# Mean squares of q and k taken token by token, with the squares as the stationary operand, in a two-layer encoder trunk

## The chip, the cores and the metric

The kernel runs on one core of a Trainium2 chip. The metric is the device time of one execution in microseconds (us), lower is better. Engines are named as in the profile: PE is TensorE's matmul, PEld its weight load, ACT is ScalarE, DVE is VectorE, POOL is GpSimd, and SP issues the DMAs.

## The reference

One sequence of 512 tokens with 1024 channels passes two residual layers. Layer 0 mixes with a gated convolution and a gated linear recurrence, layer 1 with stick-breaking attention in 16 heads of 64 channels; each is followed by an MLP with squared ReLU. The change touches only the QK-norm of layer 1:

```python
def mixer_stick_breaking(h, w_qkv, q_norm, k_norm, w_out):
    qkv = (h @ w_qkv).reshape(B, S, 3, SB_HEADS, SB_HEAD_DIM)
    q = rms_norm(qkv[:, :, 0], q_norm)
    k = rms_norm(qkv[:, :, 1], k_norm)
    ...
def rms_norm(x, g):
    y = xf * lax.rsqrt(jnp.mean(xf * xf, axis=-1, keepdims=True) + EPS)
```

So each token needs, for each head, the mean of 64 squares of q and the mean of 64 squares of k.

## The kernel before

Activations stand with channels on the 128 partitions and the 512 tokens along the columns. Weight products are written as three fp32r matmuls each (lines 281 to 283, and 1595 to 1597 for v): high part by high part, high by low, low by high. The attention layer works on pairs of heads: pair p (0 to 7) has its q in one tile of 128 channels (two heads of 64) by 512 tokens, and its k in another.

The attention stage isn't written in program order. `Graph` holds operations with an engine, a planned duration and their dependences; `Graph.run` places them one after the other by planned time, priority and ring slots, and what comes out is each engine's fixed order of instructions. A planned duration that changes can so move other operations, on any engine. Matmuls of weights form one chain that gives PE its filling; the rest, the attention units and the norms, is placed between them with priority 0 as soon as the plan says that it can start. Tiles that are used in turn come from rings: `miscs` is a ring of two PSUM banks, `nsqs` of two tiles of squares, `rows_` of one tile in SBUF.

For each pair: `q_evict` and `k_evict` take q and k out of PSUM, and among that write the squares (`nsq`, ACT). `mean_squares` forms the means and adds EPS into a 128 x 16 tile `m` of ring r0, which has tokens on the partitions and, along the columns, q or k (s), block of 128 tokens (b) and head (h). `qk_norm` takes the reciprocal root of m on DVE (`rsqrt_of`, lines 301 to 308), turns k's half back to rows and scales k. The attention units (`unit_z`, `unit_t`, `unit_a`) follow.

`mean_squares` before has four steps:

- line 1459, PE: for s = 0 and s = 1 a matmul whose stationary operand is `hs` (128 x 32, fp32: 1/64 in 16 columns for each head) and whose moving operand is the tile of squares (128 channels by 512 or 256 tokens). It leaves the means with tokens along the columns, 16 equal rows for each head, in partitions 64 to 127 of one bank. The compiler makes two matmul instructions of each such fp32 matmul.
- line 1461, ACT: a copy of these 64 rows from PSUM to the tile `rows`.
- line 1465, PE: one transpose of 64 x 128 for each block of 128 tokens, into a second bank.
- line 1468, DVE: EPS is added, and one of each 16 equal columns is kept, into m.

It is called ten times: for pairs 0 and 1 twice each with two blocks (tokens 0 to 255, then 256 to 511), and for pairs 2 to 7 once with four blocks (`qk_stream`).

Of the kernel before, what the change touches and what calls it, by code (L numbers as in the profile page):

```python
# [13 lines left out]
F32 = mybir.dt.float32  # L14
# [6 lines left out]
ALU = mybir.AluOpType  # L21
PSUM = bass.MemoryType.PSUM

P = 128
T = 512
NT = 8
EPS = 1e-6
# [184 lines left out]
def act_us(n, psum=False, column=False):  # L212

    return 0.094 + n * 0.000833 - 0.042 * psum + 0.093 * column


def dve_us(n):
    return 0.068 + n * 0.00104


def trunk(tc, x_d, c_d, rep_d, small_d, const_d, ada_d, ws_d, win_d, wv_d, woab_d, w1_d, w2_d, wqk_d, wvc_d, woc_d, out_d):
    nc = tc.nc
    act, dve, pool_e, pe, sync = nc.scalar, nc.vector, nc.gpsimd, nc.tensor, nc.sync
# [19 lines left out]
    ident = cons[:, C_ID:C_ID + P]  # L243
    ones = base.tile([P, P], F32, name="ones")
    o32 = cons[:, C_O32:C_O32 + 32]
    hs = cons[:, C_HS:C_HS + 32]
# [38 lines left out]
    def ks(k):  # L285
        return slice(k * P, (k + 1) * P)
# [975 lines left out]
    def ring(where, shape, dt, name, n=1):  # L1262

        return Ring(lambda k: (where() if callable(where) else where).tile(shape, dt, name=name, tag=name, bufs=n), n)

    def bank_ring(bs):
        r = Ring(lambda k: pp.tile([P, T], F32, name=f"b{bs[k]}", tag=f"b{bs[k]}"), len(bs))
        for k, b in enumerate(bs):
            if b in banks:
                r.slots[k] = tail[banks[b]]  # L1270
        return r
# [4 lines left out]
    miscs, accs, zts = bank_ring(free_b[:2]), bank_ring(free_b[2:4]), bank_ring(free_b[4:])  # L1276
# [7 lines left out]
    def in_ap(shape, dt, name, n=1):  # L1284
        r = ring(lambda: ap, shape, dt, name, n)
        ap_rings.append(r)
        return r
# [10 lines left out]
    oms, bes = [one_tile(om_t, i) for i in range(3)], [one_tile(be_t, i) for i in range(3)]  # L1298
    stqs, stks, kraws = in_ap([P, 1024], F32R, "stq", 5), in_ap([P, T], F32R, "stk", 6), in_ap([P, T], F32, "kraw", 3)
    vrs, oTs, krows = in_ap([P, 4, 256], F32, "v", 2), in_ap([P, T], F32R, "oT", 10), in_ap([4, T], F32R, "krow")  # L1300
    rows_ = in_ap([P, T], F32, "rows")
    rrs = [in_ap([P, 16], F32, f"r{i}", n) for i, n in enumerate((2, 1, 3, 3))]
    yts = in_ap([P, 16], F32R, "yt", 2)
    xh = {(o, hf): Handle() for o in range(NT) for hf in range(2)}
# [8 lines left out]
    def on_act(n, fn, r, w, prio=1, psum=False, column=False, **kw):  # L1313
        return G.op("ACT", act_us(n, psum, column), fn, r, w, prio, **kw)

    def on_dve(n, fn, r, w, prio=1, **kw):
        return G.op("DVE", dve_us(n), fn, r, w, prio, **kw)

    def on_pe(dur, fn, r, w, prio=0, **kw):
        return G.op("PE", dur, fn, r, w, prio, **kw)  # L1320
# [104 lines left out]
    QQ, KK, kraw, sqs, rq, oT, vs = {}, {}, {}, {}, {}, {}, {}  # L1425
# [18 lines left out]
    def k_evict(p, ps, cut, sl):  # L1444
# [4 lines left out]
        on_act(n, lambda: act.copy(kraw[p].t[:, sl], cut(ps.t)), (ps,), (kraw[p],), 0, psum=True)  # L1449
        on_act(n, lambda: act.activation(sq.t[:, sl], cut(ps.t), AF.Square), (ps,), (sq,), 0, psum=True)  # L1450

    def mean_squares(p, bs, s0):

        if bs[0] == 0:
            rq[p] = [rrs[i].new() for i in range(4)]
        ms, row, col, m = miscs.new(), rows_.new(), miscs.new(), rq[p][0]
        sl, n = slice(P * bs[0], P * bs[-1] + P), P * len(bs)
        for s in range(2):
            on_pe(0.13, lambda s=s, sq=sqs[p, s, s0]: pe.matmul(ms.t[64 + 32 * s:96 + 32 * s, sl], hs, sq.t[:, sl], start=True, stop=True),  # L1459
                  (sqs[p, s, s0],), (ms,), 0)  # L1460
        on_act(n, lambda: act.copy(row.t[64:, sl], ms.t[64:, sl]), (ms,), (row,), 0, psum=True)

        def flip():
            for b in bs:
                pe.transpose(col.t[:, 64 * b:64 * b + 64], row.t[64:, ks(b)], ident[64:, 64:])
        on_pe(0.08 * len(bs), flip, (row,), (col,), 0)
        bb = slice(bs[0], bs[-1] + 1)
        on_dve(16, lambda: dve.tensor_scalar(
            m.t.rearrange("p (s b h) -> p s b h", s=2, b=4)[:, :, bb],
            col.t[:, 0:256].rearrange("p (b s h r) -> p s b h r", b=4, s=2, h=2)[:, :, bb, :, 0], EPS, None, op0=ALU.add), (col,), (m,), 1)  # L1470

    def qk_norm(p):

# [97 lines left out]
    def qk_stream(p):  # L1571
        ops = []
        for s in range(2):
            w, ps = weights(wqk_d[p, s]), accs.new()
            ops += [mm3h(ps, whole, w, ks(k), (hh[0][k], hh[1][k]), FULL, k == 0, k == NT - 1, T) for k in range(NT)]
            (k_evict if s else q_evict)(p, ps, whole, FULL)
        mean_squares(p, (0, 1, 2, 3), 0)
        qk_norm(p)
        return ops
# [63 lines left out]
    for hf in range(2):  # L1643
        if hf:
            finish([nt_.acc[1]] + [nt_.sq[o, 1] for o in nin.direct], 1, 1, 0, (), [order[48 + 8]])
        ps = [r.new() for r in (accs, accs, zts, zts)]
        for k, s in by_half(hf, 4):
            order.append(mm3h(ps[s], half, w[s], ks(k), (hh[hf][k],), H[hf], k == 0, k == NT - 1, 256))
        for p in range(2):
            q_evict(p, ps[2 * p], half, H[hf])  # L1650
            k_evict(p, ps[2 * p + 1], half, H[hf])
            mean_squares(p, (2 * hf, 2 * hf + 1), 256 * hf)
# [11 lines left out]
    for s_ in "v0 q2 q3 u0 u1 v1 w0 q4 v2 q5 u2 q6 u3 q7 v3 u4 u6 w1 u5 u7".split():  # L1664
        n = int(s_[1])
# [140 lines left out]
```

## Time and profile before

| | |
|---|---|
| Median of 3 runs | 1243.63 us (1243.44 to 1245.4) |
| The profiled execution | 1245.21 us, of which the span from first to last instruction is 1243.4 us |
| PE busy | 1217.4 us, 98% of the span, 7649 matmul instructions |
| DVE busy | 890.5 us, 72% |
| ACT busy | 618.7 us, 50% |
| Mean granted clock of TensorE | 0.996 of full speed |
| HBM traffic | 127 GB/s over the span |

Matmuls are pipelined and the profile models their ends, so the duration of one instruction is longer than the time that it takes from PE. What a matmul takes is read from the start of it to the start of the next one. The mean squares lie between 622 and 826 us of the span.

### The profile page before, as it was taken

To read this page: it belongs to the slowest core of one execution; us is meant where nothing else is said; L and a number is where in the kernel's file an instruction comes from. 1 tells how busy PE (TensorE), PEld (TensorE's weight loads), DVE (VectorE), ACT (ScalarE), POOL (GpSimd) and SP (SyncE) were. 2 spreads that over 40 slices of the span, in tenths; PEclk is the share of its full clock that TensorE was granted. 3 is DMA by queue.
4 is the path that set the end of the run, shared out by engine and by line. 5 is a ranking of instruction groups with operands and counts; after the bars stand their busy time and mean duration, and the time that the engine had idled before them with its cause. 6 is when DMAs were issued, how large, how long until landed. Compare 5 with 4: busy or idle time off the path is not lost.

```text
span 1243.4 us, 19173 instructions
## 1 busy us (share of the span) xinstructions
PE 1217.4 (98%) x7649; PEld 1058.9 (85%) x7649; DVE 890.5 (72%) x1435; ACT 618.7 (50%) x1111; POOL 11.2 (1%) x24
## 2 busy tenths in 40 slices
PE   7999999989999999999999999999989999999998
PEld 6888877889899899898977877787878898998998
DVE  8996868769788687787857765568694585665761
ACT  4433233347256265274568655667465283472650
POOL 0000000000000000000300000000000000000000
PEclk9999999999999999999999999999999999999999
DMA  8764444623745727527332122323114223143141
GB/s 305 258 208 161 143 153 135 203 69 107 246 135 183 245 92 244 179 99 259 110 102 85 52 68 85 94 60 103 35 37 134 85 101 122 58 146 102 54 151 51
DMA packets 46618, 163.50 MB, mean 131 GB/s; under 512 B 5296, under 2 KB 6328, under 8 KB 46528
## 3 DMA queue, kind: packets, MB, share of 16 engines
q1 hardware_dynamic: 46384, 161.78, 39.5%
q8 instruction: 60, 0.98, 0.3%
q10 hardware_dynamic: 144, 0.49, 0.1%
q14 instruction: 30, 0.25, 0.1%
HBM read 155.96 MB, written 2.10 MB: 127 GB/s over the span
## 4 chain that ended last, share of the span: by engine, by line
PE 84%; DVE 8%; DMA 4%; ACT 2%; issue 1%; SPq 0%; DVEq 0%; ACTq 0%
PE b L281 20%; PE b L283 20%; PE b L282 20%; PE acc L281 3%; PE acc L283 3%; PE acc L282 3%; PE b L1539 2%; PE b L1560 1%; DMA raw<-in_ws 1%; PE b L1595 1%; PE b L1459 1%; DMA wraw<-in_w 1%; PE b L1596 1%; PE b L1597 1%; DVE wlo L272 1%
## 5 line engine op out<-in xcount | busy, mean ns | idle before, releaser
L271 ACT CAST whi<-wraw 128x1024 fp32r<-128x1024 f32 x125 | 130.0, 1048 | 217.9 <-DMA wraw<-in_w 87.7
L282 PE MATMUL b<-hidl,whi 128*128 128x512 f32 (+1 forms) x560 | 208.4, 372 | 1.0 <-DVE hidl L291 1.0
L281 PE MATMUL b<-hidh,whi 128*128 128x512 f32 (+1 forms) x560 | 208.6, 373 | 0.2
L283 PE MATMUL b<-hidh,wlo 128*128 128x512 f32 (+1 forms) x560 | 208.0, 371 | 0.0
L283 PE MATMUL b<-hh,wlo 128*128 128x256 f32 (+1 forms) x632 | 193.5, 306 | 7.1 <-DVE wlo L272 7.1
L281 PE MATMUL b<-hh,whi 128*128 128x256 f32 (+1 forms) x632 | 197.6, 313 | 2.0 <-ACT hh L1419 2.0
L282 PE MATMUL b<-hl,whi 128*128 128x256 f32 (+1 forms) x632 | 193.3, 306 | 1.2 <-DVE hl L1421 1.2
L272 DVE TENSOR_TENSOR wlo<-wraw,whi 128x1024 fp32r<-128x1024 f32 x125 | 152.1, 1222 | 58.8 <-ACT whi L271 57.6
L281 PEld LDWEIGHTS b<-hh,whi 128*128 128x128 f32 x632 | 120.4, 191 | 14.6 <-issue 7.2
L283 PEld LDWEIGHTS b<-hh,wlo 128*128 128x128 f32 x632 | 120.5, 191 | 13.3 <-DVE wlo L272 7.8
L282 PEld LDWEIGHTS b<-hl,whi 128*128 128x128 f32 x632 | 121.8, 193 | 6.2 <-DVE hl L1421 1.8
L282 PEld LDWEIGHTS b<-hidl,whi 128*128 128x128 f32 x560 | 105.6, 188 | 19.5 <-DVE hidl L291 1.6
L505 DVE SCALAR_TENSOR_TENSOR x<-b,modc,x 128x512 f32<-128x512 f32 (+1 forms) x102 | 68.2, 675 | 75.2 <-PE b L283 75.1
L281 PEld LDWEIGHTS b<-hidh,whi 128*128 128x128 f32 x560 | 105.2, 188 | 19.1 <-ACT hidh L290 1.0
L283 PEld LDWEIGHTS b<-hidh,wlo 128*128 128x128 f32 x560 | 105.2, 188 | 18.5
L419 DVE CUSTOM_DVE_ANT_0 wraw<-wraw,cb 128x1024 f32<-128x1024 f32 x80 | 97.4, 1221 | 26.3 <-DMA wraw<-in_ada 25.9
L272 DVE TENSOR_TENSOR wlo<-tt,whi 128x1024 fp32r<-128x1024 f32 x52 | 63.4, 1221 | 22.5 <-ACT whi L271 21.9
L271 ACT CAST whi<-tt 128x1024 fp32r<-128x1024 f32 x52 | 53.4, 1049 | 45.3 <-PE b L282 32.7
L1373 DVE TENSOR_TENSOR wlo<-raw,whi 128x1024 fp32r<-128x1024 f32 x34 | 41.6, 1222 | 23.6 <-ACT whi L1372 23.5
L291 DVE TENSOR_TENSOR hidl<-cm,hidh 128x256 fp32r<-128x256 f32 (+1 forms) x90 | 44.4, 510 | 18.5 <-ACT hidh L290 17.7
L281 PE MATMUL acc<-hh,whi 128*128 128x512 f32 x128 | 52.3, 408 | 0.0
L1523 DVE TENSOR_TENSOR_SCAN om<-om,pat 128x772 f32<-128x772 f32 (+2 forms) x24 | 46.5, 1936 | 5.8 <-ACT om L1519 5.8
(378 smaller groups left out, 2631.4 us busy)
## 6 DMA issues: line engine op xcount, KB each, us to landing
wraw<-in_w SPq DMA_DIRECT2D x124, 512.0 KB, 3.6
wraw<-in_ada SPq DMA_DIRECT2D x80, 512.0 KB, 4.3
eraw<-in_ada SPq DMA_DIRECT2D x16, 512.0 KB, 3.7
wraw<-in_win SPq DMA_DIRECT2D x16, 512.0 KB, 3.5
raw<-in_wqk SPq DMA_DIRECT2D x16, 512.0 KB, 4.1
raw<-in_ws SPq DMA_DIRECT2D x8, 512.0 KB, 6.0
wraw<-in_woab SPq DMA_DIRECT2D x8, 512.0 KB, 3.2
raw<-in_wvc SPq DMA_DIRECT2D x8, 512.0 KB, 3.3
```

The source lines that it names most:

```text
L271: act.copy(hi, raw)
L272: dve.tensor_tensor(lo, raw, hi.bitcast(F32), op=ALU.subtract)
L281: pe.matmul(ps, whi, h[0][:, hs], start=start, stop=False, **kw)
L282: pe.matmul(ps, whi, h[1][:, hs], start=False, stop=False, **kw)
L283: pe.matmul(ps, wlo, h[0][:, hs], start=False, stop=stop, **kw)
L291: dve.tensor_tensor(lo[:, sl], t_[:, sl], hi[:, sl].bitcast(F32), op=ALU.subtract)
L419: dve.tensor_tensor_reduce(out=raw, in0=raw, in1=cb, scale=1.0, scalar=0.0, op0=ALU.mult, op1=ALU.add, accum_out=modr[:, col:col + 1])
L505: dve.scalar_tensor_tensor(x[o][:, sl], ps, mcol(l, v, o), x[o][:, sl], op0=ALU.mult, op1=ALU.add)
L1373: on_dve(1024, lambda: dve.tensor_tensor(lo.t, raw.t, hi.t.bitcast(F32), op=ALU.subtract), (raw, hi), (lo,), 1)
L1459: on_pe(0.13, lambda s=s, sq=sqs[p, s, s0]: pe.matmul(ms.t[64 + 32 * s:96 + 32 * s, sl], hs, sq.t[:, sl], start=True, stop=True), (sqs[p, ...
L1523: on_dve(2 * nw, lambda: dve.tensor_tensor_scan(s_(), s_(), pats[i][:, ::-1], 0.0, op0=ALU.mult, op1=ALU.max), (om,), (om,), 2)
L1539: pe.transpose(tp.t[:, o_:o_ + P], be.t[:, w0:w0 + P], ident)
```

## The change

The squares become the stationary operand, a block of 128 tokens at a time, and the moving operand is two columns of `hs`, one for each head (columns 0 and 16). The product then has tokens on the partitions from the start, one column for each head, so that the copy, the tile `rows`, the second bank and the transposes go. All matmuls of a call are one operation of the plan, which needs both tiles of squares; its planned duration on PE is 0.22 us for each block of tokens, where the old steps had 0.13 us for each s and 0.08 us for each block.

```diff
-    rows_ = in_ap([P, T], F32, "rows")
...
+    hs2 = hs[:, 0:32:16]
+
     def mean_squares(p, bs, s0):
 
         if bs[0] == 0:
             rq[p] = [rrs[i].new() for i in range(4)]
-        ms, row, col, m = miscs.new(), rows_.new(), miscs.new(), rq[p][0]
-        sl, n = slice(P * bs[0], P * bs[-1] + P), P * len(bs)
-        for s in range(2):
-            on_pe(0.13, lambda s=s, sq=sqs[p, s, s0]: pe.matmul(ms.t[64 + 32 * s:96 + 32 * s, sl], hs, sq.t[:, sl], start=True, stop=True),
-                  (sqs[p, s, s0],), (ms,), 0)
-        on_act(n, lambda: act.copy(row.t[64:, sl], ms.t[64:, sl]), (ms,), (row,), 0, psum=True)
-
-        def flip():
-            for b in bs:
-                pe.transpose(col.t[:, 64 * b:64 * b + 64], row.t[64:, ks(b)], ident[64:, 64:])
-        on_pe(0.08 * len(bs), flip, (row,), (col,), 0)
+        col, m, sq = miscs.new(), rq[p][0], [sqs[p, s, s0] for s in range(2)]
+        view = lambda t_: t_.rearrange("p (s b h) -> p s b h", s=2, b=4)
+
+        def sums_of():
+            for s in range(2):
+                for b in bs:
+                    pe.matmul(col.t[:, 8 * s + 2 * b:8 * s + 2 * b + 2], sq[s].t[:, ks(b)], hs2, start=True, stop=True)
+        on_pe(0.22 * len(bs), sums_of, sq, (col,), 0)
         bb = slice(bs[0], bs[-1] + 1)
-        on_dve(16, lambda: dve.tensor_scalar(
-            m.t.rearrange("p (s b h) -> p s b h", s=2, b=4)[:, :, bb],
-            col.t[:, 0:256].rearrange("p (b s h r) -> p s b h r", b=4, s=2, h=2)[:, :, bb, :, 0], EPS, None, op0=ALU.add), (col,), (m,), 1)
+        on_dve(16, lambda: dve.tensor_scalar(view(m.t)[:, :, bb], view(col.t[:, 0:16])[:, :, bb], EPS, None, op0=ALU.add), (col,), (m,), 1)
```

## Rows read from the trace of the kernel before

**Rows 1.** Busy time by engine: attention, then the next norm; columns: length, engines, clock, DMA

```profile
620.00:830.00 210.00, 208.49 (x1336) 162.11 (x1336) 135.87 (x233) 133.52 (x265) 0.00 (x0) 1.00 0.27 81
890.00:930.00 40.00, 32.95 (x223) 30.68 (x224) 32.80 (x68) 22.64 (x51) 0.00 (x0) 0.91 0.08 27
```

**Rows 2.** Groups by line and shape, PE, 620 to 830 us

```profile
L1459 PE MATMUL b<-nsq,cons 128*32 128x512 f32 x24 | 12.6, 605 | 0.0
...
L1459 PE MATMUL b<-nsq,cons 128*32 128x256 f32 x16 | 5.0, 391 | 0.2 <-ACT nsq L1450 0.2
...
L1465 PE MATMUL b<-cons,rows 64*128 64x64 f32 x32 | 4.1, 238 | 0.0
```

**Rows 3.** Groups by line and shape, ACT, 620 to 830 us

```profile
L1461 ACT COPY rows<-b 64x512 f32<-64x512 f32 x6 | 3.5, 582 | 4.2 <-PE b L1459 4.2
L1461 ACT COPY rows<-b 64x256 f32<-64x256 f32 x4 | 1.5, 368 | 1.7 <-PE b L1459 1.7
```

**Rows 4.** Timeline of PE, sums of one tile of 512 tokens; columns: start, duration

```profile
702.79 0.28 PE L1596 MATMUL b<-wlo,hh 128*128 128x256 f32 x1
702.91 0.28 PE L1597 MATMUL b<-whi,hl 128*128 128x256 f32 x1
703.12 1.05 PE L1459 MATMUL b<-nsq,cons 128*32 128x512 f32 x2
704.10 0.39 PE L1595 MATMUL b<-whi,hh 128*128 128x256 f32 x1
704.32 0.28 PE L1596 MATMUL b<-wlo,hh 128*128 128x256 f32 x1
```

**Rows 5.** Timeline of PE, the four transposes of a call

```profile
756.27 0.28 PE L1597 MATMUL b<-whi,hl 128*128 128x256 f32 x1
756.48 0.46 PE L1465 MATMUL b<-cons,rows 64*128 64x64 f32 x4
756.87 0.39 PE L1595 MATMUL b<-whi,hh 128*128 128x256 f32 x1
757.10 0.28 PE L1596 MATMUL b<-wlo,hh 128*128 128x256 f32 x1
```

**Rows 6.** Timeline of PE, a call with two blocks: one tile's sums, later two transposes

```profile
640.99 0.28 PE L1597 MATMUL b<-whi,hl 128*128 128x256 f32 x1
641.20 0.62 PE L1459 MATMUL b<-nsq,cons 128*32 128x256 f32 x2
641.75 0.39 PE L1595 MATMUL b<-whi,hh 128*128 128x256 f32 x1
641.97 0.28 PE L1596 MATMUL b<-wlo,hh 128*128 128x256 f32 x1
...
643.09 0.34 PE L1465 MATMUL b<-cons,rows 64*128 64x64 f32 x2
```

**Rows 7.** Timeline of PE in layer 0: 16 fp32 matmuls, stationary 128 x 128, 64 columns moving

```profile
141.38 0.39 PE L283 MATMUL acc<-hh,wlo 128*128 128x512 f32 x1
141.61 1.89 PE L807 MATMUL lv<-Q,Kt 128*128 128x64 f32 x16
143.31 0.47 PE L281 MATMUL acc<-hh,whi 128*128 128x512 f32 x1
143.62 0.39 PE L282 MATMUL acc<-hl,whi 128*128 128x512 f32 x1
143.85 0.40 PE L283 MATMUL acc<-hh,wlo 128*128 128x512 f32 x1
```

**Rows 8.** Timeline of PE: fp32 matmuls of 128 columns moving, 32 columns, and 256

```profile
136.41 1.95 PE L820 MATMUL lv<-q,Kt 128*128 128x128 f32 x16
...
156.00 0.69 PE L798 MATMUL lv<-Q,Kt 128*32 128x32 f32 x16
...
603.78 0.60 PE L1406 MATMUL b<-nss,ones 128*128 128x256 f32 x2
604.21 0.59 PE L1406 MATMUL b<-nsq,ones 128*128 128x256 f32 x2
```

**Rows 9.** Who waited for whom, PE, 890 to 930 us; columns: total, times, longest

```profile
PE b L283 <- DVE wlo L272: 4.0, 1, 4.0
PE b L281 <- ACT hh L1419: 2.0, 1, 2.0
```

**Rows 10.** Busy time by engine, before and in a stretch of lower clock

```profile
889.90:893.20 3.30, 0.67 (x4) 0.43 (x4) 3.18 (x8) 1.77 (x5) 0.00 (x0) 1.00 0.00 0
893.30:896.70 3.40, 3.40 (x18) 3.40 (x17) 3.40 (x10) 1.71 (x4) 0.00 (x0) 0.50 0.00 0
```

## The prediction

> **What bounds the kernel now.** I read the busy time by stretches first, to see what limits the stage in which the change lies. From 620 to 830 us PE is busy for 208.49 of 210 us at full clock, while DVE has 135.87, ACT 133.52 and the DMA engines a share of 0.27 [rows 1]. The stage is PE's: what PE no longer does there shortens it, and what ACT no longer does shortens nothing by itself. Then I read the groups by line, to see how much of PE the mean squares are: 24 and 16 instructions of sums, 32 of transposes, 21.7 us by the busy column [rows 2]. That column rests on modelled ends, so I went to the timeline for start-to-start times, which tell what a group displaces.
>
> **What goes.** In the timeline a weight matmul with 256 moving columns starts 0.12 us after the last (702.79 to 702.91) [rows 4]. Around the sums of one tile of 512 tokens the steps are longer: from the matmul before (702.91) to the second matmul after (704.32) 1.41 us pass, of which two ordinary steps are 0.24, so the two instructions displace 1.17 us [rows 4]. This holds their own streams and about 0.1 us lost at either edge, which a reader who takes the busy column misses. The four transposes of a call, in the same way: 756.27 to 757.10 is 0.83, less 0.24 is 0.59 us [rows 5]. A full call has two tiles of sums and four transposes, which stand apart from each other in PE's order: 2 x 1.17 + 0.59 = 2.93 us. A call with two blocks: 640.99 to 641.97 is 0.98, less 0.24 is 0.74 us for one tile [rows 6]; its transposes are two fewer, and by their rows' durations (0.46 for four, 0.34 for two) these two are 0.12 us, so 0.59 - 0.12 = 0.47 [rows 5, 6]; together 2 x 0.74 + 0.47 = 1.95 us. Six full calls and four with two blocks: 6 x 2.93 + 4 x 1.95 = 25.4 us of PE go.
>
> ACT loses ten copies, 3.5 + 1.5 = 5.0 us [rows 3]. I count this at nothing: ACT is idle for a third of the stage and PE covers it. If PE were not the bound, the copies' 5.0 us would be the most that could come on top. The way from k's squares to the addition of EPS is shorter too: 1.17 us of k's sums, 0.58 of copy [rows 3] and 0.59 of transposes, 2.34 in all and what the copy stands in ACT's queue, become one run of 1.78 (below). PE hardly idles in the stage (1.5 us in 210), so an earlier start of the units has little to fill [rows 1], and this too is taken as nothing. DVE's addition of EPS stays. No DMA is added, removed or moved.
>
> **What comes.** A full call has 2 tiles x 4 blocks = 8 fp32 matmuls, and since each fp32 matmul is two instructions (24 for the 12 full tiles in rows 2), 16; a call with two blocks has 8. In all 6 x 16 + 4 x 8 = 128 instructions, each with a weight load of 128 x 128 and only two columns to move. The trace before has no matmul with two moving columns. The nearest rows are 16 fp32 instructions with the same stationary shape and 64 moving columns: from 141.38 to 143.62 pass 2.24 us, less two steps of 0.23 (the 512-column matmul before it starts 0.23 ahead) is 1.78, so 0.111 us each, with nothing lost at the edges [rows 7]. Twice the columns cost the same: 16 with 128 columns last 1.95 us against 1.89 [rows 7, 8], the difference being the tail of the last one. Below 128 columns, then, the moving side doesn't set the step; what both have in common is the load of 128 stationary columns. I take 0.111 us, and two columns instead of 64 gain nothing.
>
> Bounds for the step: from below, instructions with 32 stationary and 32 moving columns, 16 in 0.69 us; with 0.2 us as an estimate of the last one's duration, below the 0.28 of a matmul with 256 columns [rows 4], the step is (0.69 - 0.2) / 15 = 0.033 us [rows 8]. They load a quarter of the columns, so this is an end and not the value. From above, the same stationary shape with 256 columns moving: 603.78 to 604.21 for two, 0.215 us each [rows 8]. The new sums take 128 x 0.111 = 14.2 us; by the ends 4.2 and 27.5 us.
>
> [...]
>
> **The sum.** 25.4 - 14.2 = 11.2 us less on PE. The profiled execution took 1245.21 us with a span of 1243.4; it becomes a span of 1232.2 and 1234.0 us in all. The median of the runs lies 1.6 us below that execution, so 1243.6 - 11.2 = 1232.4. I say 1233, with half a microsecond for the start of the sums: all matmuls of a call are now one operation behind both squares, where q's sums went ahead alone. What is queued behind them on PE is the chain of weight matmuls and the units; the old sums waited 0.2 us for k's square in all [rows 2], and what is late next is only that wait. q's tile of squares is held until k is done. Pairs 2 to 7 have their next q many microseconds later; for pairs 0 and 1, whose four tiles become ready together, the third square can wait, a microsecond of ACT that PE's other matmuls cover, and that costs the same microsecond if they don't.
>
> **The rivals.**
>
> 1. *Given back at the seam.* The planned duration changes from 0.58 to 0.88 us a full call, and a ring slot less is taken, so the plan places other operations anew. From 890 to 930 us PE is busy for 32.95 of 40 us [rows 1], with waits of 4.0 us for a low part of weights on DVE and 2.0 for the first normalized tile [rows 9]: there the order on DVE decides and not PE. If the new order lengthens these waits, the gain shrinks by as much: waits twice as long take 6 us (1239), three times as long 12 us (1245). Speaks for it: DVE and ACT orders are fixed by the plan. Against: the work of this seam follows the last weight chain and moves with it as a whole. Time 1239 to 1248.
>
> 2. *Short steps.* If the weight load overlaps so well that two moving columns count, the step falls toward 0.033 us and the gain is 25.4 - 4.2 = 21.2: 1222.4. Rows 7 against 8 (64 and 128 columns alike) speak against it.
>
> 3. *Long steps.* If an fp32 weight load from freshly written squares can't be pulled ahead, the step is nearer 0.215 us, 25.4 - 27.5 = -2.1: 1245.7, no measurable change. Against it speak rows 7, whose stationary tile DVE writes just ahead as well (line 838), and which pay 0.111 [rows 7].
>
> [...]
>
> **How the numbers follow.** What a measurement of this kernel can tell from no change is about 0.2%, 2.5 us, so faster is below 1241.1 and slower above 1246.1. The forecast (1227 to 1239: the sum, less or more some 5 us from the new order) 0.70; seam 0.17 (0.04 still faster, 0.09 same, 0.04 slower); short steps 0.05, faster; long steps 0.03 (0.02 same, 0.01 slower); clock 0.05 (0.01 same, 0.04 slower). Faster 0.79, same 0.12, slower 0.09. For 8 in 10 I take 1226 to 1244: that leaves out short steps, long steps, the clock and about a third of the seam, 0.19.
>
> **What would show it.** In the profile after: 128 matmul instructions of sums with 128 x 2 moving, starts 0.11 us apart, and no copy and no transposes in `mean_squares`; 7649 - 72 + 128 = 7705 matmuls if nothing else changes; the end of the last call about 10 us earlier; full clock through the stage; the seam with waits of about 2 and 4 us, 11 us earlier. Steps of 0.03 or 0.2 us would make the size wrong, a fallen clock or longer waits at the seam the sign.

## The result, and the profile after

The changed kernel takes 1237.44 us (median of six runs) beside 1245.37 us for the kernel before; the ratio is 0.9942, with a 95% interval of 0.9927 to 0.9957. It is faster by about 7 us where 11 were forecast. One run of each kernel was slow (1499.59 us for the changed one, at a mean granted clock of 0.748, and 1717.87 us for the one before) and is left out of the ratio, which is one of means. The execution that was profiled here is that of 1499.59 us, so the rows of after below come from a second series of the same kernel (the first experiment: 1239.04 us beside 1244.48, ratio 0.9959, 0.9947 to 0.9971; the profiled execution 1239.04 us, span 1237.3). In that second series the gain is smaller, 5.1 us by the ratio.

Busy time by stretches of the changed kernel, columns as in [rows 1]; the second stretch is the seam of [rows 1], moved with the stage:

```profile
620.00:830.00 210.00, 206.35 (x1443) 176.63 (x1443) 143.86 (x242) 137.79 (x277) 0.00 (x0) 1.00 0.28 81
884.00:924.00 40.00, 33.14 (x224) 30.79 (x225) 34.48 (x71) 23.71 (x52) 0.00 (x0) 0.91 0.09 27
```

More work fits into the same 210 us (PE, DVE and ACT all have more instructions in it), but PE is now idle for 3.65 us of them where it was idle for 1.51 [rows 1]. The seam looks as it did: 33.1 us busy of 40, clock 0.91.

The new sums in the groups by line and shape, in place of the three lines of [rows 2]:

```profile
L1464 PE MATMUL b<-cons,nsq 128*128 128x2 f32 x128 | 15.1, 245 | 0.4 <-ACT nsq L1449 0.4
```

and one full call in the timeline of PE, to be held against [rows 4, 5]:

```profile
749.81 0.28 PE L1594 MATMUL b<-whi,hl 128*128 128x256 f32 x1
749.93 1.84 PE L1464 MATMUL b<-cons,nsq 128*128 128x2 f32 x16
751.63 0.36 PE L1592 MATMUL b<-whi,hh 128*128 128x256 f32 x1
751.83 0.28 PE L1593 MATMUL b<-wlo,hh 128*128 128x256 f32 x1
```

From 749.81 to 751.83 are 2.02 us, less two ordinary steps of 0.12 is 1.78 us for 16 instructions, 0.111 each: the price that was taken from [rows 7]. So the work went as forecast, and the missing 4 us are somewhere else. To find them, take the stage's length between two matmuls that every version has, the first and the last of the sums over channels in the norms on either side (attention's norm and the MLP's). The view of their line gives the first and last start after the durations. Before:

```profile
L1406 PE MATMUL b<-nsq,ones x16: 377/379/381, 604.2 to 899.9; 128*128 128x256 f32 x16
L1406 PE MATMUL b<-nss,ones x8: 377/380/382, 603.8 to 897.9; 128*128 128x256 f32 x8
```

After:

```profile
L1405 PE MATMUL b<-nsq,ones x16: 377/379/381, 604.3 to 893.7; 128*128 128x256 f32 x16
L1405 PE MATMUL b<-nss,ones x8: 377/379/382, 603.8 to 891.7; 128*128 128x256 f32 x8
```

603.8 to 899.9 is 296.1 us before, 603.8 to 893.7 is 289.9 after: 6.2 us less. What follows is as long as it was: the spans end 1243.4 - 899.9 = 343.5 and 1237.3 - 893.7 = 343.6 us after these marks. All of the gain, and all of what is missing, lies inside the stage. Who waited for whom on PE from 600 to 882 us, before (columns as in [rows 9]):

```profile
PE b L1539 <- DVE be L1525: 1.9, 3, 0.8
PE b L1459 <- ACT nsq L1450: 0.2, 1, 0.2
PE b L281 <- DVE x L505: 0.2, 1, 0.2
```

and after:

```profile
PE b L1536 <- DVE be L1522: 3.6, 5, 1.5
PE b L1482 <- DVE yt L1478: 0.5, 1, 0.5
PE b L1464 <- ACT nsq L1449: 0.4, 1, 0.4
PE b L1536 <- ACT whi L1371: 0.4, 1, 0.4
PE b L281 <- DVE x L505: 0.2, 1, 0.2
```

These waits total 2.3 us before and 5.1 after, and most of them stand at the transposes of the attention units (line 1536, before 1539), which the change doesn't touch. The longest, in the timeline of all engines but the weight loads:

```profile
853.10 2.28 DVE L1520 TENSOR_TENSOR_SCAN om<-om,pat 128x1026 f32<-128x1026 f32 x1
...
854.83 0.49 PE L1536 MATMUL b<-cons,be 128*128 128x128 f32 x3
855.48 1.23 DVE L1522 TENSOR_TENSOR be<-be,om 128x1025 f32<-128x1025 f32 x1
...
856.86 0.63 PE L1536 MATMUL b<-cons,be 128*128 128x128 f32 x4 [1.53 <-DVE be L1522]
857.24 0.47 PE L281 MATMUL b<-oT,whi 128*128 128x512 f32 x1
```

PE stands still for 1.53 us because the next instruction in its order is a transpose whose input DVE still multiplies, behind a scan of 2.28 us. The weight matmul that comes after the transposes (line 281) reads other tiles and doesn't wait when its turn comes; in the trace its weights were written by 851.6 us and its oT tiles by 842.2, so these operands were there before the gap began. This is a fault of the order, not of the work.

### The profile page after: what moved, and what is told of

The parts are those of the page before. It is cut to its first block, busy times and chain, and to the rows that moved or that the text cites. A ratio compares the mean times of both kernels' runs of the same rounds, so it can differ in the third digit from the quotient of the medians.

```text
span 1497.8 us, 19282 instructions
## 1 busy us (share of the span) xinstructions
PE 1481.1 (99%) x7705; PEld 1221.3 (82%) x7705; DVE 902.0 (60%) x1435; ACT 621.3 (41%) x1101; POOL 11.1 (1%) x24
## 4 chain that ended last, share of the span: by engine, by line
PE 98%; DVE 1%; DMA 1%; ACT 0%; issue 0%; SPq 0%; DVEq 0%; ACTq 0%
PE b L281 22%; PE b L283 22%; PE b L282 22%; PE acc L283 4%; PE acc L281 4%; PE acc L282 4%; PE b L1557 2%; PE b L1536 2%; PE acc L651 2%; PE b L1592 1%; PE b L1593 1%; PE b L1594 1%; PE b L1464 1%; PE b L1508 1%; PE lv L807 1%; PE b L1509 1%
## 5 line engine op out<-in xcount | busy, mean ns | idle before, releaser
L282 PE MATMUL b<-hidl,whi 128*128 128x512 f32 (+1 forms) x560 | 242.0, 432 | 0.0
L283 PE MATMUL b<-hidh,wlo 128*128 128x512 f32 (+1 forms) x560 | 241.8, 432 | 0.0
L281 PE MATMUL b<-hidh,whi 128*128 128x512 f32 (+1 forms) x560 | 241.7, 432 | 0.0
L281 PE MATMUL b<-hh,whi 128*128 128x256 f32 (+1 forms) x632 | 222.4, 352 | 2.0 <-ACT hh L1418 2.0
L283 PE MATMUL b<-hh,wlo 128*128 128x256 f32 (+1 forms) x632 | 218.8, 346 | 5.4 <-DVE wlo L272 5.4
L282 PE MATMUL b<-hl,whi 128*128 128x256 f32 (+1 forms) x632 | 218.3, 345 | 0.6 <-DVE hl L1420 0.6
L281 PEld LDWEIGHTS b<-hh,whi 128*128 128x128 f32 x632 | 137.6, 218 | 13.3 <-issue 2.2
L282 PEld LDWEIGHTS b<-hl,whi 128*128 128x128 f32 x632 | 139.3, 220 | 10.0 <-DVE hl L1420 0.9
L283 PE MATMUL acc<-hh,wlo 128*128 128x512 f32 x128 | 59.1, 461 | 0.0
L282 PE MATMUL acc<-hl,whi 128*128 128x512 f32 x128 | 58.5, 457 | 0.0
```

Of the source, the lines that this page charges most:

```text
L281: pe.matmul(ps, whi, h[0][:, hs], start=start, stop=False, **kw)
L282: pe.matmul(ps, whi, h[1][:, hs], start=False, stop=False, **kw)
L283: pe.matmul(ps, wlo, h[0][:, hs], start=False, stop=stop, **kw)
```

## The experiments

Each was timed in five rounds beside the kernel before. The stage is measured as above, in the one profiled execution of each kernel; the two pairs with the same order of PE (e1_again and e3_wide, e5_order and e9_layout) agree within 0.1 us.

| kernel | what it is | median, us | before, us | ratio (95%) | stage, us |
|---|---|---|---|---|---|
| before | old sums, old order | | | | 296.1 |
| e1_again | the change | 1239.04 | 1244.48 | 0.9959 (0.9947 to 0.9971) | 289.9 |
| e2_twice | its sums issued twice | 1262.8 | 1244.48 | 1.0146 (1.0132 to 1.0161) | 318.1 |
| e3_wide | 32 columns moving | 1239.22 | 1244.48 | 0.9961 (0.9949 to 0.9973) | 289.9 |
| e5_order | new sums, old order | 1235.14 | 1244.48 | 0.9931 (0.9916 to 0.9946) | 286.3 |
| e9_layout | the same, layout of the change | 1234.66 | 1246.88 | 0.9907 (0.9891 to 0.9923) | 286.4 |
| e6_split | two planned operations | 1239.26 | 1246.88 | 0.9948 (0.993 to 0.9966) | 290.4 |
| e4_plan | true planned duration | 1239.94 | 1246.88 | 0.9956 (0.994 to 0.9972) | 292.7 (with 3.41 us at half clock that all others but e2_twice lack) |
| e10_late | 1.4 us of planned delay | 1240.36 | 1244.54 | 0.9968 (0.9957 to 0.9978) | 291.3 |
| e11_later | 3.0 us of planned delay | 1239.3 | 1244.54 | 0.9963 (0.9948 to 0.9977) | 290.7 |
| e12_oldsums | old sums, planned anew | 1248.75 | 1244.54 | 1.0033 (1.0021 to 1.0045) | 298.6 |

The theory after the result was that the new order of the plan gives 4 us back. Its rivals were a step longer than 0.111 us and a falling clock; the 1.7 us that the expectations take for a fall are half of the 3.4 us at a granted clock of 0.50 in [rows 10].

**e1_again**, the changed kernel without an edit.

> The changed kernel as it is, for a profile at full clock. Forecast of 11.2 us, about 7 us measured; three theories for the missing 4 us. Order: the 128 matmuls take 0.11 us each and the new order of the plan gives 4 us back, so the profile shows waits of PE 4 us longer than before, and low clock only where it was before (three stretches). Clock: TensorE's clock falls to half behind some of the calls, 1.7 us each, so two or three low stretches more, between 620 and 830 us. Step: the matmuls take 0.14 us instead of 0.11 (128 x 0.03 = 4 us). Time 1236 to 1238 in each.

The step is 0.111 us, as shown above; the step theory falls. The granted clock is 1.00 from 620 to 830 us, so the clock theory falls for this kernel too. The waits of PE are 2.8 us longer, less than the 4 that order had to show; ends of matmuls are modelled and lie behind the start of the next one (0.28 us of duration beside a step of 0.12 at 749.81 us, above), and a wait shorter than such a tail isn't seen in this view. Start-to-start times show more: if each matmul is given the time since the start of the one before it, the 160 transposes of the units take 27.9 us in the change and 25.3 in e9_layout, below, which has the old order: 2.6 of the 3.5 us by which their stages differ.

**e2_twice.**

```diff
-            for s in range(2):
+            for s in (0, 1, 0, 1):
```

> The sums of each call are issued twice (same values, same order of everything else, 256 matmuls instead of 128). Order: 128 x 0.111 = 14.2 us more, 1251. Step: 128 x 0.14 = 18 us more, 1255. Clock: 14.2 us and more falls, since the runs are 3.6 us long: up to ten falls of 1.7 us less those that are there now, 1256 to 1266, with low stretches behind most calls.

23.8 us more than the change, 9.6 over the 14.2 of the step alone. In the profiled execution the stage is 28.2 us longer, 14.0 over the step, and six new stretches at a granted clock of 0.50, 30.7 us in all, lie in it. In the trace of before, weight matmuls with 256 moving columns start 0.213 us apart in the low stretch of [rows 10] (eleven steps from 893.95 to 896.29) and 0.113 apart behind it at 1.00 (six steps from 896.84 to 897.52), so about half of a low stretch is lost, as an estimate. Half of 30.7 us is 15.3, so the clock accounts for the rest to about a microsecond. (The profiled execution is the longest of the four, 1266.21 us at a mean clock of 0.981; the others have 0.985 to 0.988.) Two of the runs and the low stretches that follow them in the busy time by stretches (the clock stands third from the end):

```profile
679.07:682.56 3.49, 3.49 (x35) 3.49 (x33) 1.22 (x1) 2.10 (x5) 0.00 (x0) 1.00 0.28 70
682.60:686.00 3.40, 3.40 (x17) 2.33 (x18) 1.57 (x9) 0.31 (x1) 0.00 (x0) 0.50 0.21 82
703.67:707.80 4.13, 4.13 (x35) 4.13 (x33) 1.22 (x1) 1.52 (x3) 0.00 (x0) 0.84 0.39 127
706.50:713.30 6.80, 6.80 (x34) 6.80 (x34) 5.10 (x14) 2.70 (x5) 0.00 (x0) 0.50 0.16 55
```

PE was busy without a gap from 679.07 to 682.56 and yet the clock fell to 0.50 for the next 3.4 us; in the second run it fell 2.8 us after the run's start, for 6.8 us. At each of the six full calls of this kernel, 3.5 us long and more, the clock falls so, three times within the run and three times within 1 us after it; in the profile of the change, whose runs are half as long, at none. So the falling clock, to which the forecast gave 0.05, was measured, at runs twice as long as the change's; and the change's aren't wholly clear of it: in e4_plan, below, the clock fell once, 0.3 us behind a full call of 1.78 us.

**e3_wide.**

```diff
-                    pe.matmul(col.t[:, 8 * s + 2 * b:8 * s + 2 * b + 2], sq[s].t[:, ks(b)], hs2, start=True, stop=True)
+                    pe.matmul(col.t[:, 128 * s + 32 * b:128 * s + 32 * b + 32], sq[s].t[:, ks(b)], hs, start=True, stop=True)
```

(The addition of EPS reads one of each 16 columns.)

> The same sums with all 32 columns of hs moving instead of two of them (16 equal columns for each head, one of each kept by the addition of EPS); same number of weight loads, same order. The load of 128 columns sets the step, so order and step theories give the time of the changed kernel within 1 us (1236 to 1238). Clock theory: if it falls for want of moving columns, 16 times as many should bring fewer falls, 1233 to 1236.

The same stage to 0.1 us, 289.9: 32 moving columns take no longer than 2. With the stationary columns the step does change: a row of the trace before has the 64 moving columns of [rows 7] with half the stationary columns:

```profile
160.71 1.14 PE L798 MATMUL lv<-Q,Kt 128*64 128x64 f32 x16
```

With 0.27 us for the last one, the longest duration of its line, the step is (1.14 - 0.27) / 15 = 0.058 us with 64 stationary columns, where [rows 7] have 0.111 with 128. That it is the load of these columns which sets the step is the author's reading of such rows; no run tells the load from the rest of the matmul.

**e5_order.** The plan's operations, durations and rings are the old ones; only what they issue is new:

```diff
...
+        def sums_of(s):
+            for b in bs:
+                pe.matmul(ms.t[:, 8 * s + 2 * b:8 * s + 2 * b + 2], sq[s].t[:, ks(b)], hs2, start=True, stop=True)
+        for s in range(2):
+            on_pe(0.13, lambda s=s: sums_of(s), (sq[s],), (ms,), 0)
+        bb = slice(bs[0], bs[-1] + 1)
+        on_act(n, lambda: dve.tensor_scalar(...), (ms,), (row, m), 0, psum=True)
+        on_pe(0.08 * len(bs), lambda: None, (row,), (col,), 0)
+        on_dve(16, lambda: None, (col,), (m,), 1)
```

> The new sums in the order of before: the plan keeps the old steps and durations, q's sums stand where q's sums stood, k's where k's stood, and the copy and transposes are planned but not issued, so that every other instruction of PE, ACT and SP stands where it stood before. Order theory: the full 11.2 us come, 1233. Step theory: 7 us, 1237. Clock theory: a run is half as long (0.89 us) with ordinary matmuls between q's and k's, so few falls or none, 1233 to 1234; the profile tells it from order by the low stretches in the changed kernel.

This tells it: a stage of 286.3 us, 3.6 shorter than the change's, with the same 128 matmuls and every other instruction of PE and ACT in its old place (on DVE the additions of EPS stand somewhat earlier, where the copy was planned). The gain over before is 9.8 us of the stage.

**e9_layout**, the same without `rows_` in SBUF:

```diff
-    rows_ = in_ap([P, T], F32, "rows")
...
-        row, n = rows_.new(), P * len(bs)
+        row, n = Handle(), P * len(bs)
```

> The new sums in the order of before, as in the last run, but without the tile of rows in SBUF, so that the tiles behind it lie 2 KB lower, as in the changed kernel. Order theory: the layout does nothing, 1235 as in that run. Layout as a rival for the 3.5 us: 1238 to 1239.

286.4 us: the layout does nothing. PE's waits from 600 to 882 us are back to 2.9 us, near the 2.3 of before, with 2.3 at the transposes of the units:

```profile
PE b L1539 <- DVE be L1525: 2.1, 4, 0.8
PE b L1464 <- ACT nsq L1449: 0.4, 1, 0.4
PE b L281 <- DVE x L505: 0.2, 1, 0.2
PE b L1539 <- ACT be L1541: 0.2, 1, 0.2
```

What in the plan makes the new order worse was tried next.

**e6_split.**

```diff
...
-        on_pe(0.22 * len(bs), sums_of, sq, (col,), 0)
+        for s in range(2):
+            on_pe(0.11 * len(bs), lambda s=s: sums_of(s), (sq[s],), (col,), 0)
```

> The changed kernel with its sums as two operations of the plan, 0.11 us a block each (together the planned duration of the change), so that q's sums go ahead of k's; no planned copy. If the waits of the new order come from q's sums being held until k's square is there, most of the 3.5 us come back: 1235 to 1236. If they come from the shorter planned way (no copy and no transposes between sums and norm), they stay: 1238 to 1240.

290.4 us: q's sums ahead of k's don't bring it back.

**e4_plan.**

```diff
-        on_pe(0.22 * len(bs), sums_of, sq, (col,), 0)
+        on_pe(0.45 * len(bs), sums_of, sq, (col,), 0)
```

> The changed kernel with a planned duration of 0.45 us a block, 1.8 us for four, which is what the run takes on the chip, instead of 0.22. If a planned duration that is too short makes the new order wait, an honest one brings the 3.5 us back: 1235 to 1236. If the order is a matter of chance, anything from 1233 to 1242, with other waits at the transposes of the units.

292.7 us, but this stage holds a fall of the clock that no other but that of e2_twice has, behind one of the full calls:

```profile
678.40:680.18 1.78, 1.78 (x17) 1.76 (x16) 0.59 (x1) 0.20 (x1) 0.00 (x0) 1.00 0.19 25
680.46:683.87 3.41, 3.41 (x20) 2.79 (x17) 1.93 (x13) 0.85 (x2) 0.00 (x0) 0.50 0.35 131
```

Half of 3.41 us, the estimate used for e2_twice, is 1.7, which leaves 291.0: the true duration doesn't bring the old stage back, and its order is no worse than the others here.

**e10_late** and **e11_later** put the planned time of the copy and transposes back as a delay, 1.4 us (shown) and 3.0:

```diff
-        on_pe(0.22 * len(bs), sums_of, sq, (col,), 0)
+        on_pe(0.22 * len(bs), sums_of, sq, (col,), 0, lat=1.4)
```

> The changed kernel, with 1.4 us of planned delay between the sums and the addition of EPS, about what the planned copy and transposes took; nothing is issued for it. If the shorter planned way makes the plan place the units too early, so that PE waits at their transposes, the 3.5 us come back: 1235. If any other order than the one of before costs about as much, it stays at 1238 to 1240.

> The same with 3.0 us of planned delay. Shorter planned way as the cause: no more waits than in the order of before, 1235 or a little less. Any other order: 1237 to 1242, another scatter.

291.3 and 290.7 us: the shorter planned way by itself isn't the cause either.

**e12_oldsums** leaves the old instructions and plans them anew:

```diff
-            on_pe(0.13, lambda s=s, sq=sqs[p, s, s0]: pe.matmul(...),
+            on_pe(0.26, lambda s=s, sq=sqs[p, s, s0]: pe.matmul(...),
```

> The kernel before with one planned duration changed: 0.26 instead of 0.13 us for the sums of one tile; every instruction is the old one, only the order is planned anew. If the order of before is a lucky one and others wait more, 2 to 5 us slower than before. If only the new way of the sums makes a bad order, no change within 1.5 us.

Slower than before by 0.33%, the stage by 2.5 us, with not one instruction changed. Its largest group of waits of PE from 600 to 882 us is the known one, 4.7 us in total where before had 1.9:

```profile
PE b L1539 <- DVE be L1525: 4.7, 6, 1.4
```

So the order of before is a good one among those that the plan can make. Five other orders of the new sums cost 3.6 to 5.0 us of the stage more than it (289.9 to 291.3 against 286.3, with e4_plan taken at 291.0), and one of the old sums 2.5. What makes it good stays open: none of the three properties of the plan that were tried (the joint operation, the planned duration, the planned way to the norm) is it by itself. Not tried were their combinations, the second tile of `miscs` that the old plan takes for each call, and the time that its copy holds ACT in the plan. That its durations were fitted until the order was good would explain it, but no run shows that.

## Why the prediction was right, and where its size was off

**What bounds.** Right: what PE no longer does shortened the stage, and the 5.0 us of ACT brought nothing on top: with the order kept, the stage lost 9.8 us, no more than the PE work that was exchanged.

**What goes.** 25.4 us were forecast from three kinds of group. The same reckoning over all 29 groups in the timeline of before gives 25.2.

**What comes.** 14.2 us were forecast, 15.0 measured over the ten runs in the timeline: the step of 0.111 us from [rows 7] held, and 0.6 us is a wait inside the first call for k's square, the wait for which the prediction had held back half a microsecond. Both ends of the range of the step were far off, as their rows' other shapes had said. Two moving columns took the 0.111 us that 64 take in [rows 7], and 32 took no longer (e3_wide).

**The sum.** The exchange by itself is worth 25.2 - 15.0 = 10.2 us; with the old order kept 9.8 and 9.7 came (e5_order, e9_layout).

**The step that failed** is the one that took the new order's effect inside the stage as nothing: "PE hardly idles in the stage (1.5 us in 210), so an earlier start of the units has little to fill [rows 1], and this too is taken as nothing". The new order had a place only in the width of the forecast, some 5 us either way, and none in the sum. The step counted only what a new order could fill, not what it could open. A planned order that leaves PE idle for 1.5 us in 210 has little to win from being shuffled and much to lose. The term measured 3.6 us (289.9 against 286.3), and the gain of the stage was 6.2 us in place of about 10. That the forecast of 1227 to 1239 us still holds the result is owed to that width; the median of the second series, 1239.04 us, lies at its end.

**The rivals.** The seam (0.17) had the right mechanism, an order planned anew, at the wrong place: the waits of the seam moved with the stage, 4.0 and 2.0 us as in [rows 9] (the change, 884 to 930 us):

```profile
PE b L283 <- DVE wlo L272: 4.0, 1, 4.0
PE b L281 <- ACT hh L1418: 2.0, 1, 2.0
```

Short and long steps didn't come. The falling clock (0.05), of which [rows 10] show a case, 3.4 us at 0.50, came with runs twice as long, at all six full calls of e2_twice; with runs of 1.78 us it didn't in the profile of the change, and came once in that of e4_plan, for 3.41 us at 0.50, 1.7 us by the estimate of half.

The version to keep is that of e9_layout: the new sums in the old order, 1234.66 us, 0.93% under before (0.77% to 1.09%; 0.69% for e5_order, with the same order of PE, in another series), where the change as made has 0.41% and 0.58% in its two series.

## What to carry to other kernels

When a kernel's order comes from a planner, an edit has two prices: the work exchanged and the order drawn anew; here the first was 10.2 us and the second 3.6 back. Separate them by issuing the new instructions under the old plan's operations before the edit is judged, and keep that version if it is the better one. Cost a small group of matmuls by start-to-start times from the matmul before it to the second one after it: a third of the old transposes' price, 0.2 of 0.59 us, was at its edges.

## What the runs showed of the hardware

A group of fp32 matmuls with full 128 x 128 stationary operands displaced just its own steps (1.78 us for 16), while the old sums and transposes, whose stationary operands have 32 columns or 64 rows, lost about 0.1 us at either edge [rows 4 to 6]; why they do isn't shown. The step followed the stationary columns: 0.111 us with 128 of them and 2, 32 or 64 moving, 0.058 with 64. The granted clock fell to 0.50 at runs of 3.5 us and more of matmuls with two moving columns (e2_twice), for 3.4 or 6.8 us, in six cases of six, though PE was busy without a gap in the two that are shown (3.49 of 3.49 us and 4.13 of 4.13). Behind runs of 1.7 us it stayed at 1.00 in all six cases of e1_again and fell in one of six of e4_plan.
